# Attention output split per two head pairs, and another choice of PSUM bank for the transposed probabilities

## The chip, the cores and the metric

The kernel runs on one core of one Trainium2 chip. The metric is the device time of one execution in microseconds (us); the median of several executions stands for a kernel. The engines are named as in the profile: PE is the tensor engine's matmul, PEld its weight load, DVE the vector engine, ACT the scalar engine, POOL the GpSimd, SP the engine that issues most DMAs. PSUM has eight banks of 512 float32 values per partition; PE writes there, ACT and DVE read from there.

## What is computed

The reference is a decoder trunk of two layers over 256 tokens of width 1024: each layer is a SwiGLU feed-forward half step, a token mixer, and a second feed-forward half step. The first layer's mixer is a gated linear recurrence, the second's is attention with a forget gate. The change lies in that attention:

```
q = (xq @ w_q).reshape(Bn, S, N_HEADS, HEAD_DIM).transpose(0, 2, 1, 3) * (HEAD_DIM ** -0.5)
for blk in range(S // Q_BLOCK):
    ...
    logits = jnp.einsum('bhqd,bhkd->bhqk', q[:, :, q0:end], k[:, :, :end]).astype(jnp.float32)
    logits = logits + c[:, :, q0:end, None] - c[:, :, None, :end]
    logits = jnp.where(kpos[None, :] <= qpos[:, None], logits, -jnp.inf)
    p = jax.nn.softmax(logits, axis=-1).astype(v.dtype)
    outs.append(jnp.einsum('bhqk,bhkd->bhqd', p, v[:, :, :end]))
o = jnp.concatenate(outs, axis=2).transpose(0, 2, 1, 3).reshape(Bn, S, D_ATTN)
return o @ w_o
```

There are 16 heads of 64, that is 8 pairs of heads, and two blocks of 128 queries. Block 0 sees 128 keys, block 1 sees 256.

## The kernel before

**Numbers as two parts.** Weights and activations of the large products are split into an upper part (`hi`, fp32r) and a rest (`lo`), and a product is three matmuls (`mm3`, lines 205 to 209): upper by upper, upper by rest, rest by upper. Each weight unit of 128x1024 is loaded by SP into `raw`, copied to `whi` by ACT (line 199), and its rest goes to `wlo` by DVE (line 200). Nine units (`WB`) can be split ahead; a unit's place comes free when PE has used it for both blocks.

**Order of the work.** The order of PE's instructions is the order in which the program issues them. The queues of the other engines are put in order by a scheduler, which takes what is ready and, among that, what was issued earlier; the parts in `tc.high_priority()` (such as `enter`, lines 299 to 323) go first. Work is cut into items, one weight unit each; `slot(t, i)` issues item i for token block t (128 tokens), then `tick()` issues deferred pieces that have become due, and the preparation of coming weight units.

**The attention stage.** `ATT_ORDER` (line 1238) is an order written out by hand. A "0" or a "1" is the next item of that token block: eight items of the query projection (two tiles n=0, 1 of 512 columns, four items each), then eight items of the output projection w_o, which read `oh` and `ol`, the two parts of the attention output, one head pair per item (k = 0 to 7; the last two are done together, line 491). "a0" and "a1" are the next step of `attention(0)` and `attention(1)`. A step i holds up to three pieces, in this order on PE: values(i-3), turn(i-2), logits(i), where the number is a group of heads. Block 0 has four groups of two pairs, block 1 has eight groups of one pair.

- `logits` (lines 1157 to 1181): matmuls into banks 4 to 7, bias (DVE, 1170), maximum (DVE, 1172), exponentials (ACT, 1178), reciprocal and scaling (DVE, 1180, 1181) into `pe`.
- `turn` (1183 to 1189): four transposes of `pe` on PE into a bank of kind "mm", copied to `pT` by ACT (1189).
- `values` (1191 to 1209): matmuls with `pT` into a held bank `po`. A bank collects four pairs, 512 columns; after the fourth, ACT copies it to `oh` (1207), DVE writes the rest to `ol` (1208), and the bank is released.

**The banks.** Banks 0 to 3 are of kind "mm". `bank` (lines 67 to 76) keeps a list of them in the order in which they were handed out: it takes the free bank at the front, the one handed out longest ago, or with `again=True` the free bank at the end, and puts it at the end of the list. A bank that is held (`po`, and the accumulators of the projections) isn't free until `release`. Release is a matter of the list alone: the instruction that next writes the bank still has to wait on the chip until the last reader of the bank is done. Other takers of such banks are the query projection's accumulators (441, read by DVE into `htok`, 1027), its transposes (1030, read by ACT into `qT`, 1033), w_o's two accumulators for each block (489, read in `enter` by ACT, 248, and DVE, 314), and `rstd_rows` (294).

Followed through the code, the list stands at 2, 0, 1, 3 when the attention stage begins. In the kernel before, the transposes of block 0 take banks 0, 0, 2, 2 and all eight of block 1 take bank 2; `po` takes bank 3, then bank 0 each time; w_o's accumulators are banks 1 and 3 for both blocks.

Of the kernel before, what the change touches and what calls it, by code (L numbers as in the profile page):

```python
# [9 lines left out]
F32 = mybir.dt.float32  # L10
F32R = mybir.dt.float32r
BF16 = mybir.dt.bfloat16
AF = mybir.ActivationFunctionType
ALU = mybir.AluOpType
AX = mybir.AxisListType

P = 128
D = 1024
S = 256
# [25 lines left out]
def trunk_kernel(ctx: ExitStack, tc: tile.TileContext, A: dict, out: bass.AP):  # L45
    nc = tc.nc
# [11 lines left out]
    def nm(s):  # L58
        uid[0] += 1
        return f"{s}_{uid[0]}"  # L60
# [6 lines left out]
    def bank(kind, hold=False, again=False):  # L67

        free = [i for i in order[kind] if i not in held and i not in lent]
        i = free[-1 if again else 0]  # L70
        order[kind].remove(i)
        order[kind].append(i)
        b = pall[:, i, :]
        if hold:
            held[i] = b
        return b

    def release(*banks):
        for b in banks:
            for i in [i for i, v in held.items() if v is b]:  # L80
                del held[i]

    def mmbank():
        return bank("mm", True)
# [1041 lines left out]
    att = {}  # L1126
# [17 lines left out]
    def attention(t):  # L1144

        ap = pools["a"]
        nk = t + 1
        per = 4 // nk
        np_ = per // 2
        w = nk * P  # L1150
        box = {}
        G = NH // per

        def head(hg, b, j):
            return 2 * (hg * np_ + j) + b

        def logits(hg):
            c = 4 + (hg % 2) * 2
            lg = pall[:, c:c + 2, :S]
            for j in range(np_):  # L1160
                for b in range(2):
                    p = hg * np_ + j
                    nc.tensor.matmul(lg[:, b, j * w:(j + 1) * w], att["q"][t][b * HD:(b + 1) * HD, p, :],
                                     kv["kT"][b * HD:(b + 1) * HD, p, :w], start=True, stop=True)
            v = lg.rearrange("p b (j k) -> p j b k", j=np_)
            h0 = hg * per
            bias = att["nb"][t][:, h0:h0 + per, :].rearrange("p (j b) k -> p j b k", b=2)
            if np_ == 1:
                v, bias = lg, att["nb"][t][:, h0:h0 + per, :]
            nc.vector.tensor_tensor(v, v, bias, ALU.add)  # L1170
            mx = spool.tile([P, 4], F32, tag="mx", name=nm("mx"))[:, :per]
            nc.vector.tensor_reduce(mx, lg.rearrange("p b (j k) -> p b j k", j=np_), AX.X, ALU.max, negate=True)
            sm = spool.tile([P, 4], F32, tag="sm", name=nm("sm"))[:, :per]
            pe = box["pe", hg] = ap.tile([P, per, w], F32, tag="pe", name=nm("pe"), bufs=2)
            for b in range(2):
                for j in range(np_):
                    i = b * np_ + j
                    nc.scalar.activation(pe[:, i, :], lg[:, b, j * w:(j + 1) * w], AF.Exp, bias=mx[:, i:i + 1],
                                         accum_out=sm[:, i:i + 1])
            nc.vector.reciprocal(sm, sm)  # L1180
            nc.vector.tensor_tensor(pe, pe, sm.unsqueeze(2).to_broadcast([P, per, w]), ALU.mult)

        def turn(hg):
            tp = bank("mm", again=True)
            pev = box["pe", hg].rearrange("p a b -> p (a b)")
            for j in range(4):
                nc.tensor.transpose(tp[:, j * P:(j + 1) * P], pev[:, j * P:(j + 1) * P], ident)
            pT = box["pT", hg] = ap.tile([P, 4, P], F32, tag="pT", name=nm("pT"), bufs=2)
            nc.scalar.activation(pT.rearrange("p a b -> p (a b)"), tp, AF.Copy)

        def values(hg):
            p0 = hg * np_
            if p0 % 4 == 0:
                box["po"] = mmbank()
            po, pT = box["po"], box["pT", hg]
            for j in range(np_):
                o = (p0 + j) % 4 * P
                for k in range(nk):
                    for b in range(2):
                        hd = head(hg, b, j)  # L1200
                        nc.tensor.matmul(po[b * HD:(b + 1) * HD, o:o + P], kv["v"][k][:, hd * HD:(hd + 1) * HD],
                                         pT[:, (b * np_ + j) * nk + k, :], start=k == 0, stop=k == nk - 1)
            if (p0 + np_) % 4 == 0:
                b = (p0 + np_) // 4 - 1
                oh_v = att["oh"][t][:, 4 * b:4 * b + 4, :].rearrange("p a b -> p (a b)")
                ol_v = att["ol"][t][:, 4 * b:4 * b + 4, :].rearrange("p a b -> p (a b)")
                nc.scalar.activation(oh_v, po, AF.Copy)
                nc.vector.tensor_tensor(ol_v, po, oh_v.bitcast(F32), ALU.subtract)
                release(po)

        steps = []
        for i in range(G + 3):
            s = []
            if 0 <= i - 3 < G:
                s.append(lambda i=i: values(i - 3))
            if 0 <= i - 2 < G:
                s.append(lambda i=i: turn(i - 2))
            if i < G:
                s.append(lambda i=i: logits(i))
            steps.append(s)  # L1220
        return steps
# [13 lines left out]
    ffn_d = ffn_items(lambda: pools["f"], A["ffn2_w_gate"][1], A["ffn2_w_up"][1], A["ffn2_w_down"][1], A["ffn2_post_g"][1],  # L1235
                      lambda t, hid: None, last=True)

    ATT_ORDER = ("0 0 0 0 0 0 0 a0 0 a0 1 1 1 a0 1 1 a0 1 1 a0 1 a1 0 a0 0 a1 0 a0 0 a1 0 a1 0 a1 0 a1 0 a1 1 a1 1 a1 1 a1 1 a1 1 1 1 1")


    def half(t, i):
# [106 lines left out]
    nxt = [n_ffn3, n_ffn3]  # L1348
    for c in ATT_ORDER.split():
        if c[0] == "a":  # L1350
# [45 lines left out]
```

## Time and profile before

| | |
|---|---|
| median of 3 executions | 1005.46 us (1004.4 to 1006.44) |
| profiled execution | 1004.7 us, of which 1003.0 us are the span from the first to the last instruction |
| mean granted clock of the tensor engine | 0.998 |
| busy share of the span | PE 98%, PEld 83%, DVE 67%, ACT 56%, POOL 5% |
| DMA | 182.06 MB, 182 GB/s on average |

How to read it: a timeline row gives the start in us from the span's start, the duration, the engine, the line of the kernel, the operation, what it writes and reads, the shape, and in brackets the idle time of the engine before it with the instruction that ended the idle time. Rows of several instructions (x8) give the time of the group. Matmuls overlap: a row of 0.39 us for 512 columns can be followed by the next 0.23 us after its start, so PE's pace is read from starts. A row of groups gives the total busy time in us and the mean in ns; a row of waits gives the total in us, how often, and the longest.

### The profile page before, as it was taken

The numbers are of one execution on the slowest core, as the hardware profiler recorded it, in microseconds if no ns is written. First come the engines' busy times: TensorE is split into PE (matmuls) and PEld (weight loads), VectorE is DVE, ScalarE is ACT, GpSimd is POOL, SyncE is SP. The second block draws the span as 40 slices with busy tenths as digits, with TensorE's granted clock in tenths as the row PEclk, the third lists the DMA queues.
The fourth block names the chain that finished last, engine by engine and source line by source line (L and its number), as shares of the span: only waits on it lengthen the run. The fifth ranks groups of instructions, "written<-read, shape, count | busy, mean of one in ns | idle before, by whom it ended". The sixth has DMA issues, their size and how long they took to land.

```text
span 1003.0 us, 13842 instructions
## 1 busy us (share of the span) xinstructions
PE 984.7 (98%) x5272; PEld 834.3 (83%) x5272; DVE 675.3 (67%) x784; ACT 561.6 (56%) x732; POOL 51.5 (5%) x97
## 2 busy tenths in 40 slices
PE   8999999999999999999999999999999999999997
PEld 5888888789988888888898888888886678888886
DVE  4877664668998676664696676664488767666542
ACT  5756543559987555543565555553466656555431
POOL 1500000000003000000000000000030000000000
PEclk9999999999999999999999999999999999999999
DMA  6876645565427666545368666554485147665431
GB/s 230 288 244 215 207 156 189 161 176 152 139 81 249 217 187 185 194 162 177 114 212 277 190 176 196 194 189 151 165 294 168 43 147 252 184 194 188 157 119 42
DMA packets 94104, 182.06 MB, mean 182 GB/s; under 512 B 11838, under 2 KB 33430, under 8 KB 93910
## 3 DMA queue, kind: packets, MB, share of 16 engines
q1 hardware_dynamic: 92790, 180.06, 55.1%
q10 hardware_dynamic: 608, 1.06, 0.3%
q8 instruction: 41, 0.67, 0.3%
q0 software_dynamic: 640, 0.07, 0.1%
q14 instruction: 25, 0.20, 0.1%
HBM read 180.09 MB, written 1.06 MB: 181 GB/s over the span
## 4 chain that ended last, share of the span: by engine, by line
PE 68%; issue 22%; ACT 5%; DVE 4%; POOL 1%; DMA 0%; DVEq 0%; POOLq 0%; ACTq 0%
PE pall L233 23%; PE pall L235 12%; PE pall L207 9%; PE pall L209 9%; PE pall L208 9%; PE pall L859 1%; PE pall L214 1%; PE pall L215 1%; PE pall L216 1%; ACT junk L248 1%; DVE wlo L200 1%; ACT whi L199 1%; PE pall L257 1%; POOL rstd L243 1%; DVE h L318 1%
## 5 line engine op out<-in xcount | busy, mean ns | idle before, releaser
L200 DVE TENSOR_TENSOR wlo<-raw,whi 128x1024 fp32r<-128x1024 f32 (+4 forms) x329 | 394.6, 1206 | 248.9 <-ACT whi L199 248.0
L199 ACT ACTIVATE whi<-raw 128x1024 fp32r<-128x1024 f32 (+4 forms) x329 | 342.0, 1044 | 295.7 <-PE pall L209 114.0
L233 PE MATMUL pall<-xall,whi 128*128 128x512 f32 x1216 | 330.9, 394 | 0.0
L233 PEld LDWEIGHTS pall<-xall,whi 128*128 128x128 f32 x1216 | 208.2, 188 | 26.7
L235 PEld LDWEIGHTS pall<-xall,wlo 128*128 128x128 f32 x1216 | 186.2, 188 | 26.5
L235 PE MATMUL pall<-xall,wlo 128*128 128x256 f32 x1216 | 193.5, 281 | 0.0
L207 PE MATMUL pall<-whi,hid 128*128 128x512 f32 (+2 forms) x400 | 153.1, 383 | 0.5 <-ACT v L1110 0.5
L209 PE MATMUL pall<-whi,hid 128*128 128x512 f32 (+2 forms) x400 | 152.5, 381 | 0.0
L208 PE MATMUL pall<-wlo,hid 128*128 128x512 f32 (+2 forms) x400 | 152.5, 381 | 0.0
L207 PEld LDWEIGHTS pall<-whi,hid 128*128 128x128 f32 x400 | 75.2, 188 | 14.3 <-ACT v L1110 0.8
L209 PEld LDWEIGHTS pall<-whi,hid 128*128 128x128 f32 x400 | 75.1, 188 | 13.7
L208 PEld LDWEIGHTS pall<-wlo,hid 128*128 128x128 f32 x400 | 75.1, 188 | 13.6
L207 PE MATMUL pall<-whi,xall 128*128 128x512 f32 (+2 forms) x168 | 67.1, 399 | 0.4 <-DVE t L314 0.3
L208 PE MATMUL pall<-wlo,xall 128*128 128x512 f32 (+2 forms) x168 | 65.0, 387 | 0.4 <-DVE wlo L1259 0.2
L209 PE MATMUL pall<-whi,xall 128*128 128x512 f32 (+2 forms) x168 | 64.9, 386 | 0.1
L241 POOL TENSOR_SCALAR nv<-ss 128x1 f32<-128x1 f32 x24 | 10.2, 425 | 936.7 <-ACT junk L248 936.5
L208 PEld LDWEIGHTS pall<-wlo,xall 128*128 128x128 f32 x168 | 31.7, 189 | 7.4 <-DVE wlo L200 1.1
L209 PEld LDWEIGHTS pall<-whi,xall 128*128 128x128 f32 x168 | 31.6, 188 | 7.0 <-DVE xall L271 1.1
L207 PEld LDWEIGHTS pall<-whi,xall 128*128 128x128 f32 x168 | 31.6, 188 | 6.9 <-DVE t L314 0.7
L595 ACT ACTIVATE sil<-sil 128x1024 f32<-128x1024 f32 (+1 forms) x21 | 20.6, 980 | 23.5 <-DVE sil L594 23.5
L605 ACT ACTIVATE hid<-prod 128x1024 fp32r<-128x1024 f32 (+1 forms) x21 | 20.6, 980 | 18.9 <-DVE prod L601 18.9
L312 DVE SCALAR_TENSOR_TENSOR t<-pall,rstd,gb 128x512 f32<-128x512 f32 x16 | 11.9, 748 | 26.7 <-ACT junk L248 26.7
(192 smaller groups left out, 991.8 us busy)
## 6 DMA issues: line engine op xcount, KB each, us to landing
raw<-in_ffn_w_down_dram SPq DMA_DIRECT2D x88, 512.0 KB
raw<-in_ffn_w_up_dram SPq DMA_DIRECT2D x80, 512.0 KB
raw<-in_ffn_w_gate_dram SPq DMA_DIRECT2D x79, 512.0 KB
raw<-in_rg_w_in_dram SPq DMA_DIRECT2D x20, 504.0 KB
raw<-in_rg_w_out_dram SPq DMA_DIRECT2D x10, 504.0 KB
raw<-in_ffn_w_gate_dram SPq DMA_DIRECT2D x18, 256.0 KB
raw<-in_ffn_w_up_dram SPq DMA_DIRECT2D x16, 256.0 KB
raw<-in_w_kv_dram SPq DMA_DIRECT2D x8, 512.0 KB
```

The costliest lines, as they stand in the source:

```text
L199: nc.scalar.activation(hi[:parts, c:c + m], rawv[:, c:c + m], AF.Copy)
L200: nc.vector.tensor_tensor(lo[:parts, c:c + m], rawv[:, c:c + m], hi[:parts, c:c + m].bitcast(F32), ALU.subtract)
L207: nc.tensor.matmul(ps, xh, wh, start=first, stop=False)
L208: nc.tensor.matmul(ps, xh, wl, start=False, stop=False)
L209: nc.tensor.matmul(ps, xl, wh, start=False, stop=last)
L214: nc.tensor.matmul(ps, wh, xh, start=first, stop=False)
L233: nc.tensor.matmul(o[:, b], w, both, start=k == 0, stop=False)
L235: nc.tensor.matmul(oh[:, b], w, upper, start=False, stop=k == 7)
L241: nc.gpsimd.tensor_scalar(v, ss[:, 0:1], ss[:, 1:2] if n == 2 else 0.0, D * EPS * f * f, ALU.add, ALU.add)
L312: nc.vector.scalar_tensor_tensor(t1[n], pf[n], r_in, gb[:, n * 512:(n + 1) * 512], ALU.mult, ALU.mult)
L595: nc.scalar.activation(s, s, AF.Silu)
L605: nc.scalar.activation(hv, pv, AF.Copy)
```

## The change

Three things change. A `po` bank collects two pairs instead of four, in its first 256 columns, and is copied to `oh` and `ol` after the second: eight copies of 256 columns on ACT and eight on DVE in place of four of 512 on each. The transposes take the free bank at the front of the list instead of the one at its end. The string of `ATT_ORDER` is written in two lines, with the same content.

```
         def turn(hg):
-            tp = bank("mm", again=True)
+            tp = bank("mm")
...
         def values(hg):
             p0 = hg * np_
-            if p0 % 4 == 0:
+            if p0 % 2 == 0:
                 box["po"] = mmbank()
             po, pT = box["po"], box["pT", hg]
             for j in range(np_):
-                o = (p0 + j) % 4 * P
+                o = (p0 + j) % 2 * P
...
-            if (p0 + np_) % 4 == 0:
-                b = (p0 + np_) // 4 - 1
-                oh_v = att["oh"][t][:, 4 * b:4 * b + 4, :].rearrange("p a b -> p (a b)")
-                ol_v = att["ol"][t][:, 4 * b:4 * b + 4, :].rearrange("p a b -> p (a b)")
-                nc.scalar.activation(oh_v, po, AF.Copy)
-                nc.vector.tensor_tensor(ol_v, po, oh_v.bitcast(F32), ALU.subtract)
+            if (p0 + np_) % 2 == 0:
+                k0 = p0 + np_ - 2
+                oh_v = att["oh"][t][:, k0:k0 + 2, :].rearrange("p a b -> p (a b)")
+                ol_v = att["ol"][t][:, k0:k0 + 2, :].rearrange("p a b -> p (a b)")
+                nc.scalar.activation(oh_v, po[:, :S], AF.Copy)
+                nc.vector.tensor_tensor(ol_v, po[:, :S], oh_v.bitcast(F32), ALU.subtract)
                 release(po)
```

More of the change, by code (lines that the diff above doesn't have):

```diff
@@ L1236, in trunk_kernel @@
                       lambda t, hid: None, last=True)
-    ATT_ORDER = ("0 0 0 0 0 0 0 a0 0 a0 1 1 1 a0 1 1 a0 1 1 a0 1 a1 0 a0 0 a1 0 a0 0 a1 0 a1 0 a1 0 a1 0 a1 1 a1 1 a1 1 a1 1 a1 1 1 1 1")
+    ATT_ORDER = ("0 0 0 0 0 0 0 a0 0 a0 1 1 1 a0 1 1 a0 1 1 a0 1 a1 0 a0 0 a1 0 a0 0 a1 0 a1 0 a1 0 a1 0 a1 "
+                 "1 a1 1 a1 1 a1 1 a1 1 1 1 1")
     def half(t, i):
```

## The prediction

> **What bounds the kernel now.** I read the page's first part, then the table of windows for the attention stage (744 to 812 us: each engine's busy time, and at the end the granted clock, the DMA share and GB/s), then the waits of TensorE (PE) there, and then the timeline at each of them.
>
> ```profile
> span 1003.0 us, 13842 instructions
> PE 984.7 (98%) x5272; PEld 834.3 (83%) x5272; DVE 675.3 (67%) x784; ACT 561.6 (56%) x732; POOL 51.5 (5%) x97
> 744.00:812.00 68.00, 63.17 (x386) 44.24 (x385) 52.55 (x79) 44.98 (x111) 4.21 (x7) 1.00 0.41 132
> PE pall L209 <- DVE ol L1208: 2.8, 3, 1.7
> PE pall L207 <- ACT oh L1207: 1.0, 1, 1.0
> PE pall L1187 <- ACT qT L1033: 0.3, 1, 0.3
> PE pall L207 <- DVE t L314: 0.3, 1, 0.3
> ```
>
> PE is busy for 98% of the span, so a microsecond that PE loses is a microsecond of the kernel. In the attention stage (744 to 812) PE is idle for 4.8 us, and its waits name the places: 2.8 us for `ol`, 1.0 for `oh`, and 0.3 each for `qT` and `t`. These are the stalls that the change can remove; it leaves PE's instructions and their order alone. All that counts is which waits go, and which come. The program puts the next writer of a bank behind the last reader of it, so the banks decide.
>
> **The banks after the change**, by following the list of line 64 through `ATT_ORDER` from 2, 0, 1, 3. In t=0, turn(0) takes bank 1 (now 0), and every values(g) takes a bank that was read shortly before: values(0) takes bank 2, which q's tile t=1, n=0 has just left to `htok`. In t=1 only two banks are left beside the two accumulators of w_o. When values(1) has released its bank, that bank was handed out before the transposes' bank, so it is the oldest free one: **turn(2), the next instruction on PE, takes the very bank whose copies `oh` and `ol` have only been issued.** The same happens with values(5) and turn(6). Today all of turn(0) to turn(7) of t=1 take bank 2, whose reader is done before values. After values(3) four banks are free, and turn(4) takes w_o's old accumulator; but w_o's second accumulator for t=1 is then values(3)'s bank.
>
> **Prices of the new copies.** The four copies of 512 columns on each engine become eight of 256.
>
> ```profile
> L1207 ACT ACTIVATE oh<-pall 128x512 fp32r<-128x512 f32 x4 | 2.4, 596 | 0.0
> L297 ACT ACTIVATE rrow<-pall 128x256 f32<-128x256 f32 x5 | 1.9, 382 | 5.1 <-PE pall L295 5.0
> L1208 DVE TENSOR_TENSOR ol<-pall,oh 128x512 fp32r<-128x512 f32 x4 | 2.7, 683 | 0.0
> L937 DVE TENSOR_TENSOR y<-pall,tt 126x256 f32<-126x256 f32 x2 | 0.8, 404 | 0.0
> ```
>
> The nearest rows of 256 columns give 0.38 us (ScalarE, ACT) and 0.40 us (VectorE, DVE). ACT gains 8 x 0.38 - 4 x 0.60 = 0.7 us of work and DVE 8 x 0.40 - 4 x 0.68 = 0.5. Neither is paid directly: in the stage ACT is busy 45 of 68 us and DVE 53. It is paid where PE waits behind it.
>
> **Term 1, the first half: -0.2.**
>
> ```profile
> 752.64 0.66 PE L1187 MATMUL pall<-ident,pe 128*128 128x128 f32 x4 [0.31 <-ACT qT L1033]
> 756.45 0.74 DVE L1027 TENSOR_SCALAR htok<-pall,rstd 128x512 f32<-128x512 f32 x1
> 756.84 0.66 PE L1201 MATMUL pall<-pT,v 128*64 128x128 f32 x8
> 764.76 0.74 DVE L1027 TENSOR_SCALAR htok<-pall,rstd 128x512 f32<-128x512 f32 x1
> 765.65 0.47 PE L207 MATMUL pall<-whi,oh 128*128 128x512 f32 x1 [0.30 <-ACT pT L1189]
> 766.75 0.51 PE L209 MATMUL pall<-whi,ol 128*128 128x512 f32 x1 [0.40 <-DVE ol L1208]
> 773.10 0.66 PE L1201 MATMUL pall<-pT,v 128*64 128x128 f32 x8
> 773.69 0.50 PE L207 MATMUL pall<-whi,oh 128*128 128x512 f32 x1
> 774.02 0.39 PE L208 MATMUL pall<-wlo,oh 128*128 128x512 f32 x1
> 774.25 0.40 PE L209 MATMUL pall<-whi,ol 128*128 128x512 f32 x1
> ```
>
> The last four rows are the undisturbed pace: 0.59 us from values to the next group, then 0.33 and 0.23 from matmul to matmul. turn(0) in bank 1 no longer waits for `qT`, and its idle of 0.31 goes. But values(0) now needs bank 2, which `htok` reads until 756.45 + 0.74 = 757.19: it starts at 757.24, 0.40 late instead of early. DVE is what holds `htok` back, so what turn(0) won is lost here. At w_o's first item the accumulator (bank 3, today bank 1) is again one that `htok` reads, until 765.50; with one half of `ol` ahead of it I take 765.95, so L207 starts at 766.0 and L209 0.56 later, at 766.56 instead of 766.75, since `ol` of pairs 0 and 1 is long done. Ends: -0.5 (`htok` not delayed, L207 where it is now) to +0.2 (two halves ahead of it). The later banks of t=0, 2 and 0 by turns, are read a step before they are written again.
>
> **Term 2, turn(2) of t=1: +1.8.**
>
> ```profile
> 781.33 0.66 PE L1201 MATMUL pall<-pT,v 128*64 128x128 f32 x8
> 781.89 0.46 ACT L1178 ACTIVATE pe<-pall,mx 128x256 f32<-128x256 f32 x1
> 781.92 0.66 PE L1187 MATMUL pall<-ident,pe 128*128 128x128 f32 x4
> 782.67 0.69 DVE L1181 TENSOR_TENSOR pe<-pe,sm 128x512 f32<-128x512 f32 x1
> 783.28 0.69 DVE L1170 TENSOR_TENSOR pall<-pall,nb 128x512 f32<-128x512 f32 x1
> ```
>
> values(1) ends at 781.99. ACT is in the exponentials of an earlier step until 781.89 + 0.46 = 782.35, then copies `oh` until 782.73; DVE is in L1181, also of an earlier step, and takes its next instruction at 783.28: `ol` until 783.68. turn(2) starts at 783.73 instead of 781.92. Everything behind it on PE (logits(4), values(2), w_o's last items of t=0) moves with it, since their inputs hang on PE. Lower end, both engines free: 0.07 + 0.38 + 0.40 and three hand-overs of 0.05 = 1.0. Upper end, one more DVE step of 0.69: 2.5.
>
> **Term 3, w_o's first item of t=1: -0.6.**
>
> ```profile
> 789.32 0.68 DVE L314 TENSOR_TENSOR t<-pall,gb 128x512 f32<-128x512 f32 x1
> 789.89 0.50 PE L207 MATMUL pall<-whi,oh 128*128 128x512 f32 x1
> 790.25 1.41 DVE L318 SCALAR_TENSOR_TENSOR h<-t,rstd,h 128x512 f32<-128x512 f32 x2 [0.25 <-POOL rstd L243]
> 791.58 0.68 DVE L1208 TENSOR_TENSOR ol<-pall,oh 128x512 fp32r<-128x512 f32 x1
> 792.32 0.50 PE L209 MATMUL pall<-whi,ol 128*128 128x512 f32 x1 [1.69 <-DVE ol L1208]
> 792.65 0.39 PE L207 MATMUL pall<-whi,oh 128*128 128x512 f32 x1
> ```
>
> This is the longest stall, and it goes only in part. `ol` of pairs 0 and 1 is early now. The first accumulator is one that L314 reads until 790.00, a start 0.15 late that lies inside the wait that follows: the second accumulator (the matmul at 792.65) is in values(3)'s bank, and `ol`(3) stands in the same place behind L318, until 791.58 + 0.40 = 791.98: that matmul starts at 792.03 instead of 792.65. If `ol`(3) goes into DVE's gap ahead of L318 instead, the wait is gone and the gain is about 1.8. I take the order that the trace shows; the other end is -1.8, and -0.3 if `oh` comes late.
>
> **Term 4, turn(6): +2.3.**
>
> ```profile
> 796.83 0.66 PE L1201 MATMUL pall<-pT,v 128*64 128x128 f32 x8
> 796.94 1.06 ACT L199 ACTIVATE whi<-raw 128x1024 fp32r<-128x1024 f32 x1 [0.94 <-PE pall L209]
> 797.42 0.65 PE L1187 MATMUL pall<-ident,pe 128*128 128x128 f32 x4
> 798.02 1.23 DVE L200 TENSOR_TENSOR wlo<-raw,whi 128x1024 fp32r<-128x1024 f32 x1 [0.30 <-ACT whi L199]
> ```
>
> values(5) ends at 797.49, but ACT has begun a weight split (until 798.00), then copies until 798.38; by then DVE is in the split's other half until 799.25; `ol` ends at 799.65 and turn(6) starts at 799.70 instead of 797.42. Lower end 1.0 as above; upper end 3.5, with one more L200 (1.23) ahead.
>
> **Term 5, w_o's fifth item of t=1: -1.95.**
>
> ```profile
> 802.82 0.66 PE L1201 MATMUL pall<-pT,v 128*64 128x128 f32 x8
> 804.52 0.50 PE L207 MATMUL pall<-whi,oh 128*128 128x512 f32 x1 [1.04 <-ACT oh L1207]
> 805.19 0.68 DVE L1208 TENSOR_TENSOR ol<-pall,oh 128x512 fp32r<-128x512 f32 x1
> 805.92 0.50 PE L209 MATMUL pall<-whi,ol 128*128 128x512 f32 x1 [0.67 <-DVE ol L1208]
> ```
>
> Pairs 4 and 5 are split two steps earlier, so L209 starts at 802.82 + 0.59 + 0.56 = 803.97 instead of 805.92. Pairs 6 and 7 are needed only after 12 matmuls of 0.23 us, at 806.2, and `ol` is over by 805.87 even at full size: those matmuls hide it, and without them its 0.67 of waiting would stand again. Next late is the accumulator that L314 reads, 0.3 us, as now.
>
> **The sum** is -0.2 + 1.8 - 0.6 + 2.3 - 1.95 = +1.35 us. Against the profiled execution (1004.7 us, span 1003.0) that gives 1006.1; this execution lay 0.8 below the median of 1005.46, so I forecast 1005.46 + 1.35 = **1006.8**. All ends together give -0.5 + 1.0 - 1.8 + 1.0 - 1.95 = -2.2 and 0.2 + 2.5 - 0.3 + 3.5 - 1.95 = +4.0.
>
> **The rivals.**
> - **The copies go first, or the new waits are not there (faster).** With `oh` and `ol` at the head of both queues the sum is at its low end, 1003.2; without terms 2 and 4 it is -0.2 - 0.6 - 1.95 (-1.2 more if `ol`(3) goes first), 1001.5 to 1002.7. For it speaks that ACT is idle 0.94 us before the split at 796.94, so a little shift lets `oh` in; against it, that the split is ready 0.5 us before values(5) ends.
> - **The copies queue behind a second weight split (slower).** One place, turn(6): if L200 is followed at once by another, as DVE has them in pairs elsewhere, `ol` comes 1.23 later, term 4 is 3.5 and the time is 1008.0; it decides from 0.7 us on, where the sum passes 2 us. With term 2 also at its end it is 1008.7. For it speaks that PE's new stalls leave the splits waiting in both queues, and that a kernel at 98% PE can hide nothing; against it, that these splits are released by PE itself, at 796.94 with no other ready.
> - **Nothing to see:** terms 2 and 4 cost their lower 1.0 and term 3 gains 0.6: -0.8, 1004.7. The change would then only have moved the waits.
> - **The clock.** A stall at the upper end of term 4, 3.5 us (1008.0), would be twice the longest wait in the stage. If TensorE ran at half speed for as long after it, its matmuls would take 0.46 us apart instead of 0.23 and lose half of 3.5, 1.7 us: 1009.7. The window of the stage has the clock at 1.00, with a wait of 1.69 in it. The Trainium skill, "TensorE: Matmul & The Clock Gate", section "What's actually happening", says that an idle window of about 3.4 us brings the clock to half; no run here shows it.
>
> **How the numbers follow.** A measurement of this kernel can tell about 0.2%, 2 us, from no change. Chances: my forecast with its near ends (0 to +2) 0.35 and nothing to see 0.10, both within 0.2%; slower by a second split or more queueing 0.36, the clock 0.02; faster 0.17. So faster 0.17, same 0.45, slower 0.38. The range holds the sum's ends, rounded outward: 1002.6 to 1009.6; the likeliest case alone has 1005.5 to 1007.5.
>
> **What would show it.** In the changed profile: eight `oh` and eight `ol` of about 0.38 and 0.40 us; no wait for `qT` before L1187 and none for `oh` at w_o's fifth item of t=1; two new waits of about 1.8 and 2.3 us of L1187 for `ol` L1208; a wait of about 1.2 us of L207 for `ol` at w_o's first item of t=1; values(0) of t=0 waiting for `htok`. If L1187 shows no wait for `ol`, terms 2 and 4 are wrong and the kernel is faster. If waits appear beyond 812, the queues of ACT and DVE were reordered, and the sum is short of terms.

## The result, and the profile after

| | before | changed |
|---|---|---|
| median | 1005.08 us (1004.14 to 1007.13, 22 executions) | 1006.87 us (1005.48 to 1009.06, 22 executions) |
| profiled execution | 1004.7 us, span 1003.0 | 1006.81 us, span 1005.1 |

The ratio of the changed kernel to the one before is 1.0014, 95% interval 1.0008 to 1.0020: slower by 0.8 to 2.0 us, inside the 0.2% that the prediction called no change; the two medians are 1.8 us apart. First the changed kernel's page:

```profile
span 1005.1 us, 13850 instructions
PE 985.4 (98%) x5272; PEld 834.7 (83%) x5272; DVE 676.0 (67%) x788; ACT 562.3 (56%) x736; POOL 51.5 (5%) x97
```

Four instructions more on DVE and four on ACT, 0.7 us of work on each; PE has the same 5272 matmuls. PE's waits in the attention stage (total, times, longest, in us):

```profile
PE pall L1187 <- DVE ol L1208: 3.9, 2, 2.2
PE pall L207 <- DVE ol L1208: 1.0, 1, 1.0
PE pall L1201 <- DVE htok L1027: 1.0, 1, 1.0
PE pall L207 <- DVE t L314: 0.3, 1, 0.3
PE pall L207 <- DVE htok L1027: 0.2, 1, 0.2
```

The waits for `oh` (1.0), of L209 for `ol` (2.8), and for `qT` (0.3) are gone. In their place stand two waits of the transposes (L1187) for `ol`, one of values (L1201) for `htok`, and one for `ol` at w_o's second accumulator: 6.1 us of waiting (L314's 0.3 apart) in place of 4.4 (with the 0.3 ahead of w_o's first item). The copies, by form:

```profile
L1207 ACT ACTIVATE oh<-pall 128x256 fp32r<-128x256 f32 x8 | 3.0, 380 | 2.1 <-PE pall L1201 2.1
L1208 DVE TENSOR_TENSOR ol<-pall,oh 128x256 fp32r<-128x256 f32 x8 | 3.3, 415 | 0.0
```

The timeline of the changed kernel, in the places of the five terms:

```profile
744.08 0.72 PE L1163 MATMUL pall<-kT,qT 64*128 64x128 f32 x8
...
756.82 0.66 PE L1201 MATMUL pall<-pT,v 128*64 128x128 f32 x8 [0.98 <-DVE htok L1027]
...
766.12 0.39 PE L209 MATMUL pall<-whi,ol 128*128 128x512 f32 x1
...
780.60 0.66 PE L1201 MATMUL pall<-pT,v 128*64 128x128 f32 x8
781.61 0.38 ACT L1207 ACTIVATE oh<-pall 128x256 fp32r<-128x256 f32 x1
781.95 0.69 DVE L1181 TENSOR_TENSOR pe<-pe,sm 128x512 f32<-128x512 f32 x1
782.56 0.42 DVE L1208 TENSOR_TENSOR ol<-pall,oh 128x256 fp32r<-128x256 f32 x1
783.03 0.66 PE L1187 MATMUL pall<-ident,pe 128*128 128x128 f32 x4 [1.78 <-DVE ol L1208]
783.62 1.23 PE L1163 MATMUL pall<-kT,qT 64*128 64x256 f32 x4
784.78 1.12 PE L1201 MATMUL pall<-pT,v 128*64 128x128 f32 x8
785.83 1.12 PE L1187 MATMUL pall<-ident,pe 128*128 128x128 f32 x4
...
790.48 0.66 PE L1201 MATMUL pall<-pT,v 128*64 128x128 f32 x8
...
792.67 1.42 DVE L318 SCALAR_TENSOR_TENSOR h<-t,rstd,h 128x512 f32<-128x512 f32 x2 [0.26 <-POOL rstd L243]
794.00 0.42 DVE L1208 TENSOR_TENSOR ol<-pall,oh 128x256 fp32r<-128x256 f32 x1
794.47 0.50 PE L207 MATMUL pall<-whi,oh 128*128 128x512 f32 x1 [1.04 <-DVE ol L1208]
...
798.76 0.66 PE L1201 MATMUL pall<-pT,v 128*64 128x128 f32 x8
798.87 1.06 ACT L199 ACTIVATE whi<-raw 128x1024 fp32r<-128x1024 f32 x1 [0.94 <-PE pall L209]
799.83 0.37 ACT L1207 ACTIVATE oh<-pall 128x256 fp32r<-128x256 f32 x1
799.96 1.23 DVE L200 TENSOR_TENSOR wlo<-raw,whi 128x1024 fp32r<-128x1024 f32 x1 [0.30 <-ACT whi L199]
801.10 0.42 DVE L1208 TENSOR_TENSOR ol<-pall,oh 128x256 fp32r<-128x256 f32 x1
801.57 0.66 PE L1187 MATMUL pall<-ident,pe 128*128 128x128 f32 x4 [2.15 <-DVE ol L1208]
...
808.12 0.40 PE L209 MATMUL pall<-whi,ol 128*128 128x512 f32 x1
...
813.61 0.50 PE L207 MATMUL pall<-whi,xall 128*128 128x512 f32 x1 [0.29 <-DVE t L314]
```

Three rows of the kernel before that the prediction did not need serve as marks:

```profile
744.60 0.71 PE L1163 MATMUL pall<-kT,qT 64*128 64x128 f32 x8
...
788.09 0.66 PE L1201 MATMUL pall<-pT,v 128*64 128x128 f32 x8
...
811.50 0.50 PE L207 MATMUL pall<-whi,xall 128*128 128x512 f32 x1 [0.30 <-DVE t L314]
```

Two chains can be read off. At 781.61 ACT copies `oh` once its exponentials are through, DVE does L1181 first, `ol` is over at 782.98, and turn(2) starts 0.05 later. At 798.87 a weight split has ACT, then DVE (L200), and `ol` comes behind both. And one thing was not in the sum: behind the first wait the rows of 0.66 to 0.70 us become 1.12 to 1.23. The table of windows (the clock is the third number from the end) says why:

```profile
744.00:814.00 70.00, 63.44 (x382) 44.75 (x381) 52.69 (x83) 45.59 (x115) 4.02 (x6) 0.98 0.40 126
783.00:787.00 4.00, 3.97 (x22) 2.48 (x22) 1.39 (x2) 0.60 (x1) 0.00 (x0) 0.57 0.02 4
800.00:804.00 4.00, 2.43 (x16) 2.13 (x17) 2.28 (x4) 2.06 (x7) 0.00 (x0) 1.00 0.62 189
```

From about 783.6 to 787.0, 3.4 us, TensorE's granted clock was half. Behind the longer wait of turn(6) it stayed at 1.00 in this execution.

### The profile page after: what moved, and what is told of

Its sections match the earlier page's. It is cut to its first block, busy times and chain, and to the rows that moved or that the text cites. A ratio compares the mean times of both kernels' runs of the same rounds, so it can differ in the third digit from the quotient of the medians.

```text
span 1005.1 us, 13850 instructions
## 1 busy us (share of the span) xinstructions
PE 985.4 (98%) x5272; PEld 834.7 (83%) x5272; DVE 676.0 (67%) x788; ACT 562.3 (56%) x736; POOL 51.5 (5%) x97
## 4 chain that ended last, share of the span: by engine, by line
PE 67%; issue 22%; ACT 5%; DVE 5%; POOL 1%; DVEq 0%; POOLq 0%; ACTq 0%
PE pall L233 23%; PE pall L235 12%; PE pall L207 9%; PE pall L208 9%; PE pall L209 9%; PE pall L859 1%; DVE wlo L200 1%; PE pall L214 1%; PE pall L215 1%; PE pall L216 1%; ACT whi L199 1%; ACT junk L248 1%; POOL rstd L243 1%; ACT pe L1178 1%; DVE h L318 1%
## 5 line engine op out<-in xcount | busy, mean ns | idle before, releaser
L200 DVE TENSOR_TENSOR wlo<-raw,whi 128x1024 fp32r<-128x1024 f32 (+4 forms) x329 | 395.0, 1207 | 248.1 <-ACT whi L199 247.3
L209 PE MATMUL pall<-whi,hid 128*128 128x512 f32 (+2 forms) x400 | 152.4, 381 | 0.0
L209 PEld LDWEIGHTS pall<-whi,hid 128*128 128x128 f32 x400 | 75.1, 188 | 13.6
L209 PE MATMUL pall<-whi,xall 128*128 128x512 f32 (+2 forms) x168 | 64.9, 386 | 0.1
L209 PEld LDWEIGHTS pall<-whi,xall 128*128 128x128 f32 x168 | 31.6, 188 | 7.1 <-DVE xall L271 1.2
```

Of the source, the lines that this page charges most:

```text
L200: nc.vector.tensor_tensor(lo[:parts, c:c + m], rawv[:, c:c + m], hi[:parts, c:c + m].bitcast(F32), ALU.subtract)
L209: nc.tensor.matmul(ps, xl, wh, start=False, stop=last)
```

## The experiments

My theory: the time follows from which bank PE writes next, and who still reads it. The rival: the eight short copies load ACT and DVE, and the choice of the bank matters little. Each time below stands beside runs of the kernel before on the same chip, with a median of 1005.42 us for experiments 1 to 4, then 1004.53 (5 and 6), 1004.91 (7) and 1004.71 (8). The ratio is to these runs, with its 95% interval in brackets. The changed kernel's 1006.87 stands beside 1005.08, so the ratios (its own is 1.0014) compare better than the times.

**1. The split alone.** In the changed kernel:

```
-            tp = bank("mm")
+            tp = bank("mm", again=True)
```

> The split per two pairs alone; the transposes go on taking the last handed out free bank. Theory of the banks (what counts is which bank PE writes next): in block 1 all transposes then take one bank that is not the output's, so the waits of turn(2) and turn(6) (1.78 and 2.15 us in the changed kernel) are gone, w_o's waits too, about 3.8 us won against the kernel before; but in block 0 turn(1), turn(2) and turn(3) take the bank that values has just released, about 2.6, 2.2 and 1.2 us lost there, so 1.5 us slower than before, 1006.6, and up to 1009 if the clock drops after such waits. Rival (the eight short copies load ACT and DVE, the banks matter little): no new waits of the transposes, time as the changed kernel, 1006.9, with waits behind weight splits instead.

Measured: 1010.98 us (1010.44 to 1011.81), ratio 1.0059 (1.0044 to 1.0074). Its waits, the two longest in the timeline, and the windows behind these two:

```profile
PE pall L1187 <- DVE ol L1208: 7.1, 4, 3.0
PE pall L1201 <- DVE ol L1208: 1.3, 2, 0.7
```

```profile
760.09 1.10 PE L1187 MATMUL pall<-ident,pe 128*128 128x128 f32 x4 [3.02 <-DVE ol L1208]
...
769.69 0.66 PE L1187 MATMUL pall<-ident,pe 128*128 128x128 f32 x4 [2.75 <-DVE ol L1208]
```

```profile
760.00:764.00 4.00, 3.91 (x17) 3.08 (x18) 2.03 (x4) 0.63 (x2) 0.00 (x0) 0.57 0.71 252
770.00:774.00 4.00, 4.00 (x15) 2.36 (x13) 0.75 (x1) 1.65 (x2) 0.00 (x0) 0.57 0.69 240
```

The same eight copies cost 4 us more than in the changed kernel, because the transposes of block 0 now run into them, twice at length (3.02 and 2.75 us); and the clock falls to half after these two. The rival's 1006.9 is out. My own number was too low by 2 to 4 us: the waits were longer than I had worked out (2.6 and 2.2), and I had left the clock open.

**2. The oldest bank alone.** The kernel before, with

```
-            tp = bank("mm", again=True)
+            tp = bank("mm")
```

> The oldest free bank for the transposes alone; the output still goes out per four pairs. Theory of the banks: turn(2) of block 0 takes the bank that values(1) has just released and waits for a full oh and ol, 2.5 to 4 us; values(0) of block 0 waits about 1 us for htok; turn(0) of block 1 waits about 0.6 us; w_o's waits of block 1 (1.69, 1.04 and 0.67 us) stay. 3.5 to 4.5 us slower than before, about 1009. Rival (the short copies cost the time): with four long copies the time is that of before, 1005.1.

Measured: 1011.49 us (1009.58 to 1011.84), ratio 1.0059 (1.0044 to 1.0074). Its timeline at turn(2) of block 0, and the window there:

```profile
766.17 1.12 PE L1187 MATMUL pall<-ident,pe 128*128 128x128 f32 x4 [3.43 <-DVE ol L1208]
```

```profile
765.00:769.00 4.00, 2.83 (x9) 2.45 (x10) 1.11 (x2) 0.60 (x1) 0.00 (x0) 0.58 0.64 200
```

The wait is the one expected, 3.4 us, with the clock at half behind it. The time is not: I had expected 3.5 to 4.5 us more than before, and the ratio gives 5.9. I had no term for the clock. The profiled execution, with the one stretch at half clock, took 1009.58 us at a mean clock of 0.997; the other three took 1011.36 to 1011.84 at 0.994 or 0.995, and where they lost the rest no profile shows. Each half of the change alone costs about 6 us by the ratio, together they cost 1.4: the split makes the copies early and short, the oldest bank keeps block 0 off them, and what is left over falls on turn(2) and turn(6) of block 1.

**3. The changed kernel without these two waits.**

```
-            tp = bank("mm")
+            tp = bank("mm", again=t == 1)
```

> The changed kernel, but in block 1 the transposes take the last handed out free bank again. Theory of the banks: the two waits of turn(2) and turn(6) go (3.9 us), and w_o's first item of block 1 has no wait (1.0 us); left are values(0) of block 0 behind htok (1.0 us) and about 0.3 and 0.4 us at turn(0) and values(2) of block 1. 3 us faster than before, about 1002, ratio 0.997. Rival (the eight short copies): as the changed kernel, 1006.9, since the copies are the same.

Measured: 1002.29 us (1001.83 to 1002.67), ratio 0.9972 (0.9960 to 0.9983). Its waits:

```profile
PE pall L1201 <- DVE ol L1208: 1.2, 2, 0.6
PE pall L1201 <- DVE htok L1027: 1.0, 1, 1.0
...
PE pall L1187 <- DVE ol L1208: 0.2, 1, 0.2
```

The copies are the same eight; only the rule for the banks of block 1's transposes differs, and the kernel is 4.2 us faster than the changed one by the ratios, 4.6 by the medians. Its waits in the stage are 3.2 us in all (the three not shown are of 0.2 to 0.3) in place of 6.4, and no part of the stage is at half clock. That shows the cause: the banks that this rule hands out, and the waits and the lost clock that follow. It does not price each wait by itself, since the wait of 1.04 us at w_o's second accumulator went with the two of turn(2) and turn(6).

**4. The waits filled.** Ahead of turn(2) and turn(6) of block 1 in the changed kernel:

```
+            if t == 1 and hg in (2, 6):
+                fill = att["oh"][0]
+                for _ in range(14):
+                    nc.tensor.matmul(pall[:, 4, :S], fill[:, 0, :], fill[:, 0:2, :].rearrange("p a b -> p (a b)"),
+                                     start=True, stop=True)
             tp = bank("mm")
```

> The changed kernel with 14 matmuls of 256 columns ahead of turn(2) and of turn(6) of block 1, into a logits bank that is written anew afterwards; they fill most of the two waits and change no result. In the changed kernel's profile the granted clock is 0.50 from about 783.6 to 787.0, after turn(2)'s wait of 1.78 us, and the way from turn(2) to w_o's next matmul takes 4.50 us instead of 3.21. If the idle PE is what makes the clock drop: no such stretch here, and 1.3 us less than the changed kernel where that has it, about 1005.6. If the drop has another cause: it stays, 1006.9 or a little more.

Measured: 1005.88 us (1005.35 to 1006.58), ratio 1.0001 (0.9992 to 1.0010). The matmuls ahead of turn(2), and the window there:

```profile
782.07 1.93 PE L1187 MATMUL pall<-oh 128*128 128x256 f32 x14
```

```profile
783.00:787.00 4.00, 3.95 (x33) 2.66 (x31) 2.25 (x4) 1.00 (x2) 0.00 (x0) 1.00 0.00 0
```

turn(2) starts 2.43 us after values(1), as in the changed kernel, but PE works meanwhile, and the clock stays at 1.00. All ten executions have a mean clock of 0.998 or 0.999; of the changed kernel's 22, eighteen have 0.997 or less. So it is the idle PE that brings the clock down, and it cost the changed kernel's median about 1 us. The mean clock is taken over the whole span: it says that the clock fell, and not where. The profiled execution of experiment 3 has 0.997 too, with its low clock in the first 20 us of the span (0.90 and 0.92 in stretches of 10 us).

**5. Both rules.** The changed kernel with

```
-            tp = bank("mm")
+            tp = bank("mm", again=t == 1 and hg > 0)
...
-                box["po"] = mmbank()
+                box["po"] = bank("mm", True, again=True)
```

> The changed kernel with two rules in place of one: output banks are always the free bank handed out last (that of the transposes whose copy values needs anyway), and in block 1 so are the transposes' banks except the first. Theory of the banks: of the waits left with the transposes' rule alone (values(0) of block 0 behind htok 1.0 us, values(2) and values(6) of block 1 behind ol 0.6 each, turn(0) 0.2) all go; htok at w_o's first item (0.2) and L314 (0.3) stay. About 1.5 to 2 us less than with that rule alone (1002.3), so 1000.3 to 1000.8, unless what turn(0) wins at DVE's queue is lost again at w_o's first item, then 1001.5. Rival (short copies): no change against 1002.3, or 1006.9.

Measured: 1001.00 us (1000.59 to 1001.01), ratio 0.9961 (0.9947 to 0.9976): the best of all, and faster than both kernels. Its waits:

```profile
PE pall L1187 <- DVE pe L1181: 0.6, 1, 0.6
PE pall L207 <- DVE htok L1027: 0.4, 1, 0.4
PE pall L1201 <- ACT pT L1189: 0.4, 1, 0.4
PE pall L207 <- DVE t L314: 0.3, 1, 0.3
PE pall L1187 <- DVE htok L1027: 0.3, 1, 0.3
```

No wait for an output bank is left; those that remain are 2.0 us in all. I had expected 1000.3 to 1000.8. turn(1) of block 0 still meets `htok` (0.3), and behind the waits that went, waits of the attention's own chains stand, for `pe` (0.6) and `pT` (0.4), for which I had no term.

**6 to 8. Does the clock fall in the kernel before as well?** Its 61 executions beside these experiments come in two groups, 39 at 1004.1 to 1005.2 us with a mean clock of 0.998 or 0.999, and 22 at 1005.6 and more with 0.995 to 0.997. Three kernels fill its waits in the same way, ahead of w_o's matmuls of block 1:

```
+                    if att and "oh" in att and t == 1 and kk in (0, 4) and n == 0 and nk == 8:
...
+                        filled(2 * kk)
+                        nc.tensor.matmul(acc[t][n], xh, uu.hi[:, :512], start=kk == 0, stop=False)
+                        nc.tensor.matmul(acc[t][n], xh, uu.lo[:, :512], start=False, stop=False)
+                        filled(13 if kk == 0 else 6)
+                        nc.tensor.matmul(acc[t][n], xl, uu.hi[:, :512], start=False, stop=False)
```

The first (6) fills only the wait at kk = 0, the second (7) only those at kk = 4, the third (8) both (shown).

> The kernel before with 13 matmuls of 256 columns in its longest wait of the stage (1.69 us, ahead of the third matmul of w_o's first item of block 1), into a logits bank that is written anew afterwards; they change no result. The kernel before has executions at 1004.3 to 1005.1 us with a mean granted clock of 0.998 or 0.999, and others at 1005.7 to 1008.2 with 0.995 to 0.997. If the clock also drops there, in some executions, after that wait: the second group shrinks or goes, and the median is about 1004.5. If the second group has another cause (another place, or chance): both groups stay, in the same shares, median about 1005.3.

Measured, the first: 1004.65 us (1004.11 to 1006.67), ratio 1.0002 (0.9993 to 1.0011); 4 of 11 executions have 0.997 or less, with 4 of 14 of the kernel before beside them. The theory of one place fell.

> The kernel before with matmuls of 256 columns in the two waits of w_o's fifth item of block 1 (8 ahead of the 1.04 us wait, 6 ahead of the 0.67 us wait), into a logits bank that is not read afterwards before it is written anew; they change no result. Filling the 1.69 us wait left the second group of executions (1005.7 us and more, mean clock 0.995 to 0.997) as it was. If these two waits, 1.7 us within 2.5, are the place where the clock drops: the second group goes, median about 1004.4. If not: it stays at about a third of the executions, and the place stays open.

Measured, the second: 1005.97 us (1004.16 to 1006.85), ratio 1.0001 (0.9991 to 1.0012); 7 of 12 executions have 0.997 or less, with 7 of 17 of the kernel before beside them. That theory fell too, but this kernel's profile shows the clock low, behind the 1.69 us wait that the first had filled (L1222 is the line of `ol` here):

```profile
PE pall L209 <- DVE ol L1222: 2.1, 2, 1.7
```

```profile
788.00:792.00 4.00, 2.59 (x19) 1.43 (x18) 3.50 (x7) 2.25 (x7) 0.97 (x2) 1.00 0.00 0
792.00:796.00 4.00, 3.71 (x17) 2.26 (x18) 2.44 (x4) 2.86 (x7) 1.02 (x3) 0.60 0.01 2
```

> The kernel before with both places filled: 13 matmuls in the 1.69 us wait of w_o's first item of block 1, and 8 and 6 in the two waits of its fifth item; they change no result. With only the fifth item's waits filled, a profile showed the clock at 0.50 from about 792.9 to 796.1, right behind the 1.69 us wait; with only that wait filled, a third of the executions still had the low mean clock. If either place can make the clock drop: with both filled the second group of executions is gone, all of them at 1004.1 to 1005.2 with 0.998 or 0.999. If the stage's waits are not the whole cause: some executions stay at 1006 with 0.996.

Measured, the third: 1004.41 us (1004.13 to 1005.48), ratio 0.9995 (0.9986 to 1.0005); none of 11 executions is below 0.998, with 3 of 14 of the kernel before beside them. So it seems that either place can bring the clock down, in some executions, and the two together fit all of the second group. For the first item's place the profile above shows it; for the fifth item's place it is inferred from the counts, and no profile shows it. That the filling is what holds the clock, and not the changed time of what follows, is likely: experiment 4 points the same way with turn(2) at an unchanged distance. But eleven executions are few.

## Why the prediction was right, and where it was not

The forecast was +1.35 us and 1006.8; measured were 1006.87 and a ratio that gives +1.4. The agreement is better than the sum deserves, since one term was missing, and that the times meet within 0.1 us is luck: I had added to 1005.46, the median of three executions, where 22 have 1005.08, and 1005.08 + 1.35 would have been 1006.4. From one profiled execution to the other it was +2.1: +2.63 in the stage, and -0.52 won ahead of it. Point by point, as the shift of PE's starts from before to after, from one mark to the next (at 744 the changed execution was 0.52 early; turn(2), for instance, starts at 783.03 for 781.92, +1.11, after values(1) at 780.60 for 781.33, -0.73, which makes +1.84):

| from | to | predicted | measured |
|---|---|---|---|
| logits(0) of block 0 | L209 of w_o's first item of block 0 (term 1) | -0.2 | -0.11 |
| | values(1) of block 1 | 0 | -0.10 |
| | turn(2) (term 2) | +1.8 | +1.84 |
| | values(3) of block 1 (clock) | 0 | +1.28 |
| | second accumulator of w_o's first item (term 3) | -0.6 | -0.57 |
| | values(5) | 0 | +0.11 |
| | turn(6) (term 4) | +2.3 | +2.22 |
| | L209 of w_o's fifth item (term 5) | -1.95 | -1.95 |
| | first matmul of the feed-forward | 0 | -0.09 |
| sum | | +1.35 | +2.63 |

- **The banks** were right in every place: turn(2) and turn(6) wait for `ol`, values(0) for `htok`, w_o's second accumulator for `ol`(3), and nothing appears beyond 812. Experiment 3 has the same eight copies and other banks, and is 2.8 us faster than the kernel before by the ratio: the copies by themselves aren't the cost, the waits at the banks are.
- **Term 1** was right as a balance: turn(0) starts early, values(0) waits 0.98 for `htok`, and `ol`'s early half wins it back.
- **Terms 2 and 4** were sized by the order of the queues, not by the shortest chain of 1.0 us, and that held within 0.1 us: in both places the work that was ready earlier went first on ACT and DVE (L1181 ahead of `ol` at 781.95, the weight split ahead of `oh` at 798.87). The rival of a second weight split did not come.
- **Term 3** came as in the trace of before: `ol`(3), at 794.00, stands behind L318, which began at 792.67, and not in the gap ahead of it.
- **The clock** is the step that failed. I gave it 0.02 and tied it to a wait of 3.5 us. It fell after a wait of 1.78 us and cost 1.28 us in the profiled execution; by their mean clock, most executions (18 of 22) seem to have lost as much. The half clock lasted 3.4 us, which agrees with the window that the Trainium skill names ("TensorE: Matmul & The Clock Gate", section "What's actually happening"); that an idle stretch of that whole length is needed does not agree, and the measurement decides. My argument against it, a wait of 1.69 at a clock of 1.00, rested on one execution: the second kernel of experiments 6 to 8 has that very wait with the clock at 0.60 behind it.
- **Why the total still fits:** the kernel before has the same kind of loss in some of its executions, and its profiled one had none in the stage. Compared at a mean clock of 0.998 or 0.999, the changed kernel's four executions (1005.48 to 1005.85) stand about 1.2 us above the median of eight of the kernel before (1004.25 to 1005.12, median 1004.5; they ran beside experiments 1 to 4 and not beside the changed kernel): about the sum without the clock.

## What to carry to other kernels

The buffer handed out longest ago is not the one that has been free longest: one that is held for two steps is at the front of the list the moment it is released, with its readers still to come. Follow the list by hand through the program order, and give the next writer a bank whose reader the step needs anyway, as `pT` here. And price a wait for a copy by what stands in the copying engine's queue at that moment, not by the copy.

## What the runs showed that I had not expected

A single wait of PE of under 2 us can cost more than its length: the granted clock went to half for 3.4 us after waits of 1.78 us (changed kernel), 1.69 us (kernel before with its later waits filled), 3.02 and 2.75 us (the split alone), and 3.43 us (the oldest bank alone). It did not after one of 2.15 us in the changed kernel, nor after the one of 1.69 us in the profiled execution of the kernel before. The mean clocks say that it differs from execution to execution; what decides it stays open. Experiment 8 makes it likely that this is what spreads the kernel before over 1004.1 to 1008.2 us. The two kernels without waits of that length stay within 1 us, in seven and five executions (1001.83 to 1002.67, 1000.59 to 1001.01). The two with all of these waits filled with matmuls whose result nobody reads stay within 1.4 (1004.13 to 1005.48, 1005.35 to 1006.58).
